# Norm sums with split operands, and three weight blocks in the front, in a one-core decoder layer

## The chip, the core and the metric

The kernel runs on one core of a Trainium2 chip. A core has five engines that matter here, each with its own instruction queue, worked off in order: TensorE (PE, matrix products, with PEld for the load of the stationary operand), VectorE (DVE), ScalarE (ACT), GpSimd (POOL) and SyncE (SP), which here only starts transfers. Transfers between the chip's main memory and the core's own memory run on 16 DMA engines. The metric is the device time of one execution in microseconds, the median of several runs; smaller is better.

Two number formats appear. f32 is full single precision. f32r is a 32-bit format of reduced precision that TensorE takes at its ordinary rate. Writing a value x to an f32r tile rounds it (the high part, `hi`); `lo` is x - `hi`, written to another f32r tile. A product of two numbers is then taken as hi*hi + hi*lo + lo*hi, three f32r matmuls.

## The reference

One layer of a decoder for 256 prompt positions and 8 x 4 sample positions, 288 columns in all, with d_model 2048 and d_ff 5632. Cut to what matters:

```python
z = einsum('ntd,de->nte', x, w_in)          # one input projection: h, Bg, Cg, q, k, v, two gates
ya = gate_b * conv3(gate_c * h)             # mixer A
yb = dilated_window_attention(q, k, v)      # mixer B, three head groups
mixed = sigmoid(g_a) * (ya @ w_branch_a) + sigmoid(g_b) * (yb @ w_branch_b)
x1 = layernorm(ALPHA * x + mixed @ w_out, ln1_g, ln1_b)
a, b = split(x1 @ w_up)
y = layernorm(ALPHA * x1 + (silu(conv3(a)) * b) @ w_down, ln2_g, ln2_b)
```

The layer norm takes mean and variance over the 2048 features of each position. Features lie on the 128 partitions, 16 blocks of them, and positions along a row, so a sum over features is a sum over 16 blocks and then over partitions; the latter is a matmul with a matrix of equal entries.

## The kernel before

**Products.** Every weight matrix is cut into blocks of 128 output features: 128 partitions by 16 k-slices of 128, 1 MB in f32. `prepare()` loads the next block of `weight_list()` into one of three `wst` buffers by an SP transfer (L167), and `half_block` splits it in two halves of eight k-slices: ScalarE casts the high part to `whi` (L138), VectorE subtracts for `wlo` (L139); there are four buffers of each. `product(x)` takes a prepared block and issues for each k three matmuls into an accumulator of 288 columns (L208 to L210), 48 in all. There are five accumulators (`acc`). The order of instructions on each engine is made by a scheduler, except where `behind(a, b)` puts a behind b.

**The front.** While the inputs arrive there is nothing to multiply with, so the first two blocks of `w_in` (0 and 1) are handled apart. `FIRST` cuts the 16 k-slices into six pieces: four of two and two of four. For each piece one transfer brings its x slices (288 or 576 KB; the first four on ScalarE's queue, the others on SP's; L242) and one the same k of both blocks (256 or 512 KB, SP, L243). `split` makes high and low parts of both (L214 on ScalarE, L215 on VectorE). `first_two()` prepares block 2 by `prepare()` and multiplies piece by piece: for each piece the terms hi*hi, hi*x-low and lo*hi, over the piece's k and both blocks (L262). Then block 2 follows as an ordinary product. A warm-up of 18 matmuls on zeros (L227) runs ahead of all that. SP's transfers of the front wait for an earlier one by a semaphore: eight are under way at a time.

**The norm.** `Norm` keeps two running sums, s1 of the values and s2 of their squares. `first()` runs after feature block 0: a matmul with `ones_p` (1/128 everywhere, L610) gives the mean of block 0 for each position, which is copied to `c` (L611) and subtracted from all blocks, so that s1 and s2 stay small. `add(i)` squares a block on ScalarE (L618) and adds it to the sums on GpSimd (L622, L623). For the last block it does not add: two matmuls with `ones_d` (1/2048) take s1 and s2 (L630), and two more take the last block and its square into the same accumulators (L631). All of these ones-matmuls are in f32. `finish()` for norm 1 then forms mean and 1/r on ScalarE and VectorE (L639 to L647). The products that follow the first norm start on values that aren't normalized yet; `normed` (L712 to L715) applies 1/r to their result, so TensorE need not wait for it, but the accumulators are released only then. `finish_out()` for norm 2 is the tail of the kernel.

Of the kernel before, what the change touches and what calls it, by code (L numbers as in the profile page):

```python
# [11 lines left out]
F32R = mybir.dt.float32r  # L12
AF = mybir.ActivationFunctionType
ALU = mybir.AluOpType
# [3 lines left out]
P = 128  # L18
D = 2048
KD = D // P  # L20
# [3 lines left out]
T = SEQ + NS  # L24


H = T // 2
# [4 lines left out]
HK = KD // 2  # L32
# [24 lines left out]
R_LN = R_WCF + KF * 3  # L57
# [4 lines left out]
NB_QKV = 3 * NG * NH  # L62
# [21 lines left out]
def layer_kernel(ctx: ExitStack, tc: tile.TileContext, ins, outs):  # L84
    nc = tc.nc
    pe, dve, act, pool, sp = nc.tensor, nc.vector, nc.scalar, nc.gpsimd, nc.sync

    big = ctx.enter_context(tc.tile_pool(name="big", bufs=1))
    wp = ctx.enter_context(tc.tile_pool(name="wp", bufs=3))
    wk = ctx.enter_context(tc.tile_pool(name="wk", bufs=2))  # L90
# [4 lines left out]
    def nm(s):  # L95
        uid[0] += 1
        return f"{s}_{uid[0]}"

    def sb(pl, shape, tag, dt=F32, bufs=None):
        return pl.tile(shape, dt, tag=tag, name=nm(tag), bufs=bufs)  # L100

    def acc(half=H):
        return sb(ps, [P, half, 2], "acc")
# [4 lines left out]
    def h3(ap):  # L108
        return ap.rearrange("p k (h a) -> p k h a", h=2)

    def att(cols=512):
        return sb(ps, [P, cols], "att", bufs=2)

    def f32(ap):
        return ap.bitcast(F32)
# [9 lines left out]
    def behind(i, after):  # L125

        tc.add_manual_dep(i.ins, after.ins.name, no_sync, reason="pace")
# [12 lines left out]
        return hi, lo, n  # L140

    def weight_list():
        for b in range(2, NB_QKV + 3 * KD):
            yield ins["w_in"][b], KD
        for gate, w, nk in ((0, "w_a", KD), (KD, "w_b", NH)):
            for i in range(KD):
                yield ins["w_in"][NB_QKV + 3 * KD + gate + i], KD
                yield ins[w][i], nk
        for i in range(KD):
            yield ins["w_out"][i], KD  # L150
        f = wd = 0
        for nf in THIRDS:
            for _ in range(2 * nf):
                yield ins["w_up"][f], KD
                f += 1
            for _ in range(KD):
                yield ins["w_down"][wd : wd + nf * P * P].rearrange("(p c) -> p c", p=P), nf
                wd += nf * P * P

    w_left = weight_list()  # L160

    def prepare():
        src, nk = next(w_left, (None, 0))
        if nk == 0:
            return
        st = sb(wp, [P, KD, P], "wst")
        d = sp.dma_start(st[:, :nk, :], src.rearrange("p (k c) -> p k c", c=P))  # L167
        loads[0] += 1
        n = loads[0]
        w_load[0] = d  # L170
        if n > NB_QKV + 5 * KD and n % 11 in (0, 4, 8):
            copy_rest(d)
        w_ready.append([half_block(st, k0, min(HK, nk - k0)) for k0 in range(0, nk, HK)])
# [13 lines left out]
    def product(x):  # L187

        w = w_ready.pop(0)
        if not w_ready:  # L190
            prepare()
        if steps_on[0]:
            spent[0] += N_STEP
            while spent[0] >= N_STEP_BLOCKS:
                spent[0] -= N_STEP_BLOCKS
                next(steps, None)
        o = acc(x[0].shape[-1])
        mms(o, w, x)
        prompt_step()
        return o.rearrange("p a h -> p h a")  # L200
# [10 lines left out]
                k += 1  # L211

    def split(hi, lo, src):
        act.copy(hi, src)  # L214
        dve.tensor_tensor(lo, src, f32(hi), ALU.subtract)  # L215

    ones_d = sb(big, [P, P], "ones_d")
    ones_p = sb(big, [P, P], "ones_p")
    pool.memset(ones_d, 1.0 / D)
    pool.memset(ones_p, 1.0 / P)  # L220


    zero = sb(wk, [P, T], "cy", F32R, bufs=2)
# [1 line left out]
    o = sb(ps, [P, T], "acc")  # L225
# [4 lines left out]
    xh = sb(big, [P, KD, 2, HX], "xh", F32R)  # L230
    xl = sb(big, [P, KD, 2, HX], "xl", F32R)
    x_in = ins["x"].rearrange("p (k t) -> p k t", t=T)
    xs = sb(big, [P, KD, T], "yah")

    w_ready = []
    w_two = sb(big, [P, 2, KD, P], "dd")
    w_two_hi = sb(big, [P, 2, KD, P], "yal", F32R)
    w_two_lo = [sb(wk, [P, 2, HK, P], "cache", F32R, bufs=2) for _ in range(2)]
    w_in_two = ins["w_in"][0:2].rearrange("b p (k c) -> p b k c", c=P)
    for k0, n, queue in FIRST:  # L240
        k = slice(k0, k0 + n)
        (act if queue == "act" else sp).dma_start(xs[:, k], x_in[:, k])  # L242
        sp.dma_start(w_two[:, :, k], w_in_two[:, :, k])  # L243
    for k0, n, _ in FIRST:
        k = slice(k0, k0 + n)
        split(xh[:, k, :, :H], xl[:, k, :, :H], h3(xs[:, k]))
        split(w_two_hi[:, :, k], w_two_lo[k0 // HK][:, :, k0 % HK : k0 % HK + n], w_two[:, :, k])
    x = (xh[:, :, :, :H], xl[:, :, :, :H])
    x_gb = (xh[:, :, :, :HG], xl[:, :, :, :HG])

    def first_two():

        prepare()
        o = [acc() for _ in range(2)]
        before = None
        for k0, n, _ in FIRST:
            for term in range(3):
                for k in range(k0, k0 + n):
                    xk = x[term == 1][:, k].rearrange("p h a -> p a h")
                    for b in range(2):  # L260
                        w = w_two_lo[k // HK][:, b, k % HK] if term == 2 else w_two_hi[:, b, k]
                        i = pe.matmul(  # L262
                            o[b], w, xk, start=k == 0 and term == 0, stop=k == KD - 1 and term == 2
                        )
                        if before is not None:
                            behind(i, before)
                        before = i
        return [t.rearrange("p a h -> p h a") for t in o]
# [37 lines left out]
    def prompt_attention(j, qT, kT, vT):  # L306
# [46 lines left out]
        ])  # L353
        act.copy(oT, po)
        split(ybh[:, j, :SEQ], ybl[:, j, :SEQ], oT)


# [27 lines left out]
    def pick_t(out, p, add):  # L385

        for t in range(NT):
            dve.scalar_tensor_tensor(
                out, p[:, t * P : (t + 1) * P], tmask[:, t : t + 1], add if t == 0 else out, ALU.mult, ALU.add
            )  # L390
# [94 lines left out]


    kv = sb(big, [P, 2, 2, NG, T], "dd")
    q_first = first_two()
    for j in range(NH):
        for g in range(NG):  # L490
            act.copy(h2(q_all[:, j, g]), q_first.pop(0) if q_first else product(x))
            if j == 1:
                dst, src = ((cst, ins["cst"][:, :C_M0]), (m_dist, ins["cst"][:, C_M0:]), (prm, ins["prm"]))[g]
# [58 lines left out]
    for i in range(KD):  # L552
        ph = product(x)
        h = sb(wk, [P, T], "h", bufs=2)
# [12 lines left out]
        ya = sb(wk, [P, T], "ya", bufs=2)  # L567
# [6 lines left out]
    for i in range(KD):  # L574
# [3 lines left out]
        o = product((h3(yah), h3(yal)))  # L578
# [6 lines left out]
    for i in range(KD):  # L585
# [3 lines left out]
        o = product((h3(ybh), h3(ybl)))  # L589
# [6 lines left out]
    dd = sb(big, [P, KD, T], "dd")  # L596

    lw = sb(wk, [P, 7, T], "cache", bufs=2)

    class Norm:  # L600


        def __init__(self, g, b):
            self.g, self.b = g, b
            self.s1, self.s2, self.c = (lw[:, k] for k in range(3))

        def first(self):

            p = att(T)
            pe.matmul(p, ones_p, dd[:, 0], start=True, stop=True)  # L610
            act.copy(self.c, p)  # L611
            dve.tensor_tensor(dd[:, 0], dd[:, 0], self.c, ALU.subtract)

        def add(self, i):
            d = dd[:, i]
            last = i == KD - 1
            q = self.s2 if i == 0 else sb(wk, [P, T], "cy", bufs=2)
            act.activation(q, d, AF.Square)  # L618
            if i == 0:
                pool.tensor_copy(self.s1, d)  # L620
            elif not last:
                pool.tensor_tensor(self.s1, self.s1, d, ALU.add)  # L622
                pool.tensor_tensor(self.s2, self.s2, q, ALU.add)  # L623
            if i == KD - 2:

                act.activation(lw[:, 3, 0:1], q[:, 0:1], AF.Abs_reciprocal_sqrt)
            if last:
                self.p1, self.p2 = att(T), att(T)
                for p, s, e in ((self.p1, self.s1, d), (self.p2, self.s2, q)):
                    pe.matmul(p, ones_d, s, start=True, stop=False)  # L630
                    pe.matmul(p, ones_d, e, start=False, stop=True)  # L631

        def at(self, c, i):
            return prm[:, c + i : c + i + 1]
# [51 lines left out]
                sp.dma_start(out[:, k0 : k0 + n, :], y[:, k0 : k0 + n, :])  # L686


    n1 = Norm(R_LN, R_LN + KD)
    for i in range(KD):  # L690
        o = product((h3(mxh), h3(mxl)))
        xf = sb(wk, [P, T], "h", bufs=2)
# [25 lines left out]

    cf = sb(big, [P, KF, 2 + 2 * NB], "qk_s")
    f = 0  # L720
    n2 = Norm(R_LN + 2 * KD, R_LN + 3 * KD)
    for part, nf in enumerate(THIRDS):
        gh = sb(big, [P, KD, T], "yah", F32R)
        gl = sb(big, [P, KD, T], "yal", F32R)
# [30 lines left out]
        for i in range(KD):  # L755
            o = product((h3(gh), h3(gl)))
# [197 lines left out]
```

## Time and profile before

| | us |
|---|---|
| median of 3 runs | 1764.37 (1764.05 to 1764.5) |
| the profiled execution's own time | 1764.45 |
| its span, first to last instruction | 1762.7 |
| TensorE busy | 1744.4 |
| VectorE, ScalarE, GpSimd busy | 1008.0, 797.3, 254.1 |
| moved by DMA | 436.25 MB, mean 247 GB/s |
| granted TensorE clock, mean | 0.997 |

In the rows of the profile "start us, us, engine line op out<-in xcount" tells when an instruction (or a run of equal ones) began, how long it lasted, which engine and which line of the program it belongs to, and what it wrote from what; in brackets stands how long its engine was idle before it and what released it. TensorE's matmuls overlap one another, so the distance between two starts, not the printed 0.29 us, is what one takes. In a row of a window ("from:to length, ...") stand the busy time and count of PE, PEld, DVE, ACT and POOL, the granted clock, the share of the DMA engines in use and GB/s. A row of the waits has the total, the number and the longest. A row of transfers has count, size and median time from issue to landing.

### The profile page before, as it was taken

The numbers are of one execution on the slowest core, as the hardware profiler recorded it, in microseconds if no ns is written. First come the engines' busy times: TensorE is split into PE (matmuls) and PEld (weight loads), VectorE is DVE, ScalarE is ACT, GpSimd is POOL, SyncE is SP. The second block draws the span as 40 slices with busy tenths as digits, with TensorE's granted clock in tenths as the row PEclk, the third lists the DMA queues.
The fourth block names the chain that finished last, engine by engine and source line by source line (L and its number), as shares of the span: only waits on it lengthen the run. The fifth ranks groups of instructions, "written<-read, shape, count | busy, mean of one in ns | idle before, by whom it ended". The sixth has DMA issues, their size and how long they took to land.

```text
span 1762.7 us, 33587 instructions
## 1 busy us (share of the span) xinstructions
PE 1744.4 (99%) x14275; PEld 1713.7 (97%) x14275; DVE 1008.0 (57%) x1317; ACT 797.3 (45%) x1167; POOL 254.1 (14%) x401
## 2 busy tenths in 40 slices
PE   9999999999999999999999999999999999999996
PEld 9999999999999999999999999999999999999996
DVE  5444455555555444455588788774555554555564
ACT  5444444333434333344455655553444443345444
POOL 0000000000000000001155233310011110011174
PEclk9999999999999999999999999999999999999998
DMA  8477787787787887467766566656565666666653
GB/s 325 173 287 266 270 299 297 266 324 295 273 332 282 306 314 264 150 247 260 282 233 221 220 230 217 237 216 236 218 237 218 236 219 234 220 234 221 237 198 108
DMA packets 60198, 436.25 MB, mean 247 GB/s; under 512 B 7184, under 2 KB 8336, under 8 KB 16016
## 3 DMA queue, kind: packets, MB, share of 16 engines
q1 hardware_dynamic: 58320, 429.40, 66.2%
q10 hardware_dynamic: 1728, 4.72, 0.7%
q8 instruction: 111, 1.82, 0.4%
q14 instruction: 39, 0.32, 0.0%
HBM read 389.89 MB, written 94.53 MB: 275 GB/s over the span
## 4 chain that ended last, share of the span: by engine, by line
PE 97%; DMA 1%; ACT 1%; DVE 1%; POOL 0%; issue 0%; SPq 0%; ACTq 0%; DVEq 0%
PE acc L208 31%; PE acc L209 31%; PE acc L210 31%; PE long L407 1%; PE long L460 1%; DMA wst<-in_w_in 1%; PE att L348 0%; DMA dd<-in_w_in 0%; PE att L312 0%; ACT whi L138 0%; POOL qk_s L535 0%; ACT yah L685 0%; DVE dd L661 0%; ACT xh L214 0%; PE att L340 0%; PE att L332 0%
## 5 line engine op out<-in xcount | busy, mean ns | idle before, releaser
L139 DVE TENSOR_TENSOR wlo<-wst,whi 128x1024 fp32r<-128x1024 f32 (+1 forms) x580 | 711.1, 1227 | 617.8 <-ACT whi L138 610.8
L138 ACT CAST whi<-wst 128x1024 fp32r<-128x1024 f32 (+1 forms) x580 | 592.0, 1022 | 877.1 <-PE acc L209 769.5
L208 PE MATMUL acc<-xh,whi 128*128 128x288 f32 (+1 forms) x3232 | 928.0, 287 | 0.0
L210 PE MATMUL acc<-xh,wlo 128*128 128x288 f32 (+1 forms) x3232 | 925.4, 286 | 0.1
L209 PE MATMUL acc<-xl,whi 128*128 128x288 f32 (+1 forms) x3232 | 925.0, 286 | 0.0
L208 PEld LDWEIGHTS acc<-xh,whi 128*128 128x128 f32 x3232 | 610.8, 189 | 8.0 <-ACT cy L519 2.5
L210 PEld LDWEIGHTS acc<-xh,wlo 128*128 128x128 f32 x3232 | 610.8, 189 | 1.2 <-issue 0.8
L209 PEld LDWEIGHTS acc<-xl,whi 128*128 128x128 f32 x3232 | 610.9, 189 | 0.4 <-issue 0.2
L208 PE MATMUL acc<-yah,whi 128*128 128x288 f32 x1216 | 348.2, 287 | 0.3 <-ACT yah L214 0.3
L210 PE MATMUL acc<-yah,wlo 128*128 128x288 f32 x1216 | 347.8, 286 | 0.0
L209 PE MATMUL acc<-yal,whi 128*128 128x288 f32 x1216 | 347.6, 286 | 0.0
L208 PEld LDWEIGHTS acc<-yah,whi 128*128 128x128 f32 x1216 | 229.7, 189 | 3.2 <-ACT h L577 2.5
L210 PEld LDWEIGHTS acc<-yah,wlo 128*128 128x128 f32 x1216 | 229.8, 189 | 0.1
L209 PEld LDWEIGHTS acc<-yal,whi 128*128 128x128 f32 x1216 | 229.8, 189 | 0.1
L535 POOL COPY qk_s<-u 128x2 f32<-128x2 f32 x44 | 41.8, 949 | 573.7 <-ACT u L735 441.5
L521 DVE SCALAR_TENSOR_TENSOR cy<-u,prm,cy 128x304 f32<-128x304 f32 x120 | 70.7, 589 | 3.1 <-ACT cy L519 0.4
L592 POOL TENSOR_TENSOR ya<-ya,dd 128x288 f32<-128x288 f32 x16 | 13.6, 852 | 306.0 <-DVE ya L591 306.0
L546 DVE TENSOR_TENSOR ya<-cy,acc 128x144 f32<-128x144 f32 x132 | 25.6, 249 | 33.6 <-PE acc L210 33.6
L535 POOL COPY cm<-u 128x2 f32<-128x2 f32 x16 | 3.0, 187 | 254.1 <-DVE u L560 254.1
L214 ACT CAST yah<-ya 128x288 fp32r<-128x288 f32 x76 | 32.7, 431 | 14.0 <-POOL ya L592 8.8
L215 DVE TENSOR_TENSOR yal<-ya,yah 128x288 fp32r<-128x288 f32 x76 | 34.9, 459 | 1.3 <-ACT yah L214 1.2
L622 POOL TENSOR_TENSOR cache<-cache,dd 128x288 f32<-128x288 f32 x28 | 27.7, 988 | 46.6 <-DVE dd L701 31.5
(166 smaller groups left out, 812.4 us busy)
## 6 DMA issues: line engine op xcount, KB each, us to landing
wst<-in_w_in SPq DMA_DIRECT2D x114, 1024.0 KB, 6.0
wst<-in_w_up SPq DMA_DIRECT2D x88, 1024.0 KB, 4.8
wst<-in_w_down SPq DMA_DIRECT2D x32, 1024.0 KB, 4.9
cache<-in_ck SPq DMA_DIRECT2D x18, 1024.0 KB, 6.4
out_o_ck<-cache SPq DMA_DIRECT2D x18, 1024.0 KB, 9.3
cache<-in_cv SPq DMA_DIRECT2D x18, 1024.0 KB, 6.3
out_o_cv<-cache SPq DMA_DIRECT2D x18, 1024.0 KB, 9.9
wst<-in_w_a SPq DMA_DIRECT2D x16, 1024.0 KB, 4.9
```

The lines of the kernel that those rows point to most:

```text
L138: act.copy(hi[:, :n, :], st[:, k0 : k0 + n, :])
L139: dve.tensor_tensor(lo[:, :n, :], st[:, k0 : k0 + n, :], f32(hi[:, :n, :]), ALU.subtract)
L208: pe.matmul(out, hi[:, c, :], xh_k, start=k == 0, stop=False)
L209: pe.matmul(out, hi[:, c, :], xl_k, start=False, stop=False)
L210: last_mm[0] = pe.matmul(out, lo[:, c, :], xh_k, start=False, stop=k == nk - 1)
L214: act.copy(hi, src)
L215: dve.tensor_tensor(lo, src, f32(hi), ALU.subtract)
L407: row.append(pe.matmul(p[j * NS : (j + 1) * NS], qm[:, j, b, :], c[:, o + j * cols : o + (j + 1) * cols], start=b == 0, stop=b == NB - 1,))
L521: dve.scalar_tensor_tensor(y, u[:, i : i + YW], prm[:, w0 + i : w0 + i + 1], y, ALU.mult, ALU.add)
L535: pool.tensor_copy(dst[:, 0:2], u[:, SEQ : SEQ + 2])
L546: dve.tensor_tensor(a, b, c, ALU.mult)
L622: pool.tensor_tensor(self.s1, self.s1, d, ALU.add)
```

## The change

Two edits that do not touch one another.

The front takes three blocks instead of two. Block 2 gets a `wst` buffer of its own and two `whi` and `wlo` buffers, as it would have had from `prepare()`, but it is loaded in the same six pieces, a transfer of 128 or 256 KB behind each piece of blocks 0 and 1, and split piece by piece. `first_three()` multiplies all three blocks within each term. The splits' order (x, blocks 0 and 1, block 2, piece after piece) is fixed on ScalarE and on VectorE by `behind`. `prepare()`, called at the head of it, now loads block 3.

The norm's matrices of ones are stored as f32r. `first()` casts block 0 to f32r first and multiplies the high part alone. In norm 1 (`tail` False) `add` puts the last block into s1 and s2 as well, splits both sums at once (a cast and a subtract of 128 x 576) and issues four f32r matmuls, high parts and then low parts. Norm 2 (`tail` True) keeps its four f32 matmuls on the last block.

```diff
-        for b in range(2, NB_QKV + 3 * KD):
+        for b in range(3, NB_QKV + 3 * KD):
...
     def split(hi, lo, src):
-        act.copy(hi, src)
-        dve.tensor_tensor(lo, src, f32(hi), ALU.subtract)
-
-    ones_d = sb(big, [P, P], "ones_d")
-    ones_p = sb(big, [P, P], "ones_p")
-    pool.memset(ones_d, 1.0 / D)
-    pool.memset(ones_p, 1.0 / P)
+        return act.copy(hi, src), dve.tensor_tensor(lo, src, f32(hi), ALU.subtract)
+
+    ones_d = sb(big, [P, P], "ones_d", F32R)
+    ones_p = sb(big, [P, P], "ones_p", F32R)
+    pool.memset(f32(ones_d), 1.0 / D)
+    pool.memset(f32(ones_p), 1.0 / P)
...
+    w_one = sb(wp, [P, KD, P], "wst")
+    w_one_hi, w_one_lo = ([sb(wp, [P, HK, P], n, F32R, bufs=4) for _ in range(2)] for n in ("whi", "wlo"))
+    w_in_one = ins["w_in"][2].rearrange("p (k c) -> p k c", c=P)
     for k0, n, queue in FIRST:
         k = slice(k0, k0 + n)
         (act if queue == "act" else sp).dma_start(xs[:, k], x_in[:, k])
         sp.dma_start(w_two[:, :, k], w_in_two[:, :, k])
+        sp.dma_start(w_one[:, k], w_in_one[:, k])
+    splits = []
     for k0, n, _ in FIRST:
         k = slice(k0, k0 + n)
-        split(xh[:, k, :, :H], xl[:, k, :, :H], h3(xs[:, k]))
-        split(w_two_hi[:, :, k], w_two_lo[k0 // HK][:, :, k0 % HK : k0 % HK + n], w_two[:, :, k])
+        splits.append(split(xh[:, k, :, :H], xl[:, k, :, :H], h3(xs[:, k])))
+        h = slice(k0 % HK, k0 % HK + n)
+        splits.append(split(w_two_hi[:, :, k], w_two_lo[k0 // HK][:, :, h], w_two[:, :, k]))
+        splits.append(split(w_one_hi[k0 // HK][:, h], w_one_lo[k0 // HK][:, h], w_one[:, k]))
+    for before, after in zip(splits, splits[1:]):
+        for i in range(2):
+            behind(after[i], before[i])
...
-    def first_two():
+    def first_three():
 
         prepare()
-        o = [acc() for _ in range(2)]
+        o = [acc() for _ in range(3)]
+
+        def first_w(lo, b, k):
+            if b < 2:
+                return w_two_lo[k // HK][:, b, k % HK] if lo else w_two_hi[:, b, k]
+            return (w_one_lo if lo else w_one_hi)[k // HK][:, k % HK]
...
-                    for b in range(2):
-                        w = w_two_lo[k // HK][:, b, k % HK] if term == 2 else w_two_hi[:, b, k]
+                    for b in range(3):
                         i = pe.matmul(
-                            o[b], w, xk, start=k == 0 and term == 0, stop=k == KD - 1 and term == 2
+                            o[b], first_w(term == 2, b, k), xk, start=k == 0 and term == 0, stop=k == KD - 1 and term == 2
                         )
...
         def first(self):
 
+            hi = sb(wk, [P, T], "ya", F32R, bufs=2)
+            act.copy(hi, dd[:, 0])
             p = att(T)
-            pe.matmul(p, ones_p, dd[:, 0], start=True, stop=True)
+            pe.matmul(p, ones_p, hi, start=True, stop=True)
...
-            elif not last:
+            elif not last or not self.tail:
                 pool.tensor_tensor(self.s1, self.s1, d, ALU.add)
                 pool.tensor_tensor(self.s2, self.s2, q, ALU.add)
...
-                for p, s, e in ((self.p1, self.s1, d), (self.p2, self.s2, q)):
-                    pe.matmul(p, ones_d, s, start=True, stop=False)
-                    pe.matmul(p, ones_d, e, start=False, stop=True)
+                if self.tail:
+                    for p, s, e in ((self.p1, self.s1, d), (self.p2, self.s2, q)):
+                        pe.matmul(p, f32(ones_d), s, start=True, stop=False)
+                        pe.matmul(p, f32(ones_d), e, start=False, stop=True)
+                else:
+                    w = sb(wk, [P, 4, T], "cache", F32R, bufs=2)
+                    split(w[:, 0:2], w[:, 2:4], lw[:, 0:2])
+                    for k in range(4):
+                        pe.matmul((self.p1, self.p2)[k % 2], ones_d, w[:, k], start=k < 2, stop=k >= 2)
...
-    n1 = Norm(R_LN, R_LN + KD)
+    n1 = Norm(R_LN, R_LN + KD, False)
...
-    n2 = Norm(R_LN + 2 * KD, R_LN + 3 * KD)
+    n2 = Norm(R_LN + 2 * KD, R_LN + 3 * KD, True)
```

More of the change, by code (lines that the diff above doesn't have):

```diff
@@ L487, in layer_kernel @@
     kv = sb(big, [P, 2, 2, NG, T], "dd")
-    q_first = first_two()
+    q_first = first_three()
     for j in range(NH):
@@ L600, in layer_kernel, with __init__ @@
     class Norm:
-        def __init__(self, g, b):
-            self.g, self.b = g, b
+        def __init__(self, g, b, tail):
+            self.g, self.b, self.tail = g, b, tail
             self.s1, self.s2, self.c = (lw[:, k] for k in range(3))
         def first(self):
+            hi = sb(wk, [P, T], "ya", F32R, bufs=2)
+            act.copy(hi, dd[:, 0])
             p = att(T)
-            pe.matmul(p, ones_p, dd[:, 0], start=True, stop=True)
+            pe.matmul(p, ones_p, hi, start=True, stop=True)
             act.copy(self.c, p)
```

## The prediction

> **What bounds the kernel now.** I read the page's engine rows first, then the chain that ended last, then TensorE's waits, then the order of time at the two places that the edit touches.
>
> ```profile
> span 1762.7 us, 33587 instructions
> PE 1744.4 (99%) x14275; PEld 1713.7 (97%) x14275; DVE 1008.0 (57%) x1317; ACT 797.3 (45%) x1167; POOL 254.1 (14%) x401
> PE 97%; DMA 1%; ACT 1%; DVE 1%; POOL 0%; issue 0%; SPq 0%; ACTq 0%; DVEq 0%
> PE acc L262 <- ACT yal L214: 1.2, 2, 0.7
> PE acc L208 <- ACT yah L214: 0.3, 1, 0.3
> 26.32:1745.34 1719.02, 1718.67 (x14107) 1690.22 (x14105) 982.25 (x1284) 772.42 (x1129) 245.28 (x387) 1.00 0.67 247
> ```
>
> TensorE sets the end: 97% of the chain is its matmuls, and the last row, a window from 26.32 to 1745.34 us, shows it busy for 1718.67 of 1719.02 us at granted clock 1.00, DMA engines 67% used. A matmul taken out of that window shortens the run by its own length, and so does an earlier start of the window; VectorE (57%), ScalarE (45%) and GpSimd (14%) count only where TensorE waits for them. It waits at the front:
>
> ```profile
> 5.01 0.67 ACT L214 CAST xh<-yah 128x576 fp32r<-128x576 f32 x1 [0.96 <-DMA yah<-in_x]
> 6.26 0.76 PE L262 MATMUL acc<-xh,yal 128*128 128x288 f32 x4 [0.74 <-ACT yal L214]
> 8.18 0.75 DVE L215 TENSOR_TENSOR xl<-yah,xh 128x576 fp32r<-128x576 f32 x1
> 12.97 1.05 ACT L214 CAST yal<-dd 128x1024 fp32r<-128x1024 f32 x1 [0.16 <-DMA dd<-in_w_in]
> 14.06 1.25 PE L262 MATMUL acc<-xh,yal 128*128 128x288 f32 x8 [0.42 <-ACT yal L214]
> 15.73 1.05 ACT L214 CAST yal<-dd 128x1024 fp32r<-128x1024 f32 x1 [0.16 <-DMA dd<-in_w_in]
> 18.23 2.00 ACT L138 CAST whi<-wst 128x1024 fp32r<-128x1024 f32 x2 [1.45 <-DMA wst<-in_w_in]
> 20.05 0.29 PE L208 MATMUL acc<-xh,whi 128*128 128x288 f32 x1
> 20.58 0.39 PE L210 MATMUL acc<-xh,wlo 128*128 128x288 f32 x1
> 20.81 0.29 PE L208 MATMUL acc<-xh,whi 128*128 128x288 f32 x1
> 22.27 1.99 ACT L138 CAST whi<-wst 128x1024 fp32r<-128x1024 f32 x2 [1.45 <-DMA wst<-in_w_in]
> 26.32 0.29 PE L208 MATMUL acc<-xh,whi 128*128 128x288 f32 x1
> ```
>
> Blocks 0 and 1 run from 6.26 to 20.05, block 2 from 20.05 to 26.32, where block 3 begins. From 20.81 to 26.32 are 15 k of three matmuls: 5.51 / 45 = 0.1224 us a matmul. Three blocks are 144 matmuls, 17.63 us; back to back from 6.26 they would end at 23.89. So 26.32 - 23.89 = 2.43 us of idle TensorE is all that the front can give.
>
> **The change, the norm.** The rows show a true f32 ones-matmul between ordinary ones, at the first and at the last feature block of norm 1:
>
> ```profile
> 876.50 0.46 DVE L695 SCALAR_TENSOR_TENSOR dd<-h,acc 128x288 f32<-128x288 f32 x1 [0.30 <-PE acc L210]
> 879.11 0.29 PE L210 MATMUL acc<-yah,wlo 128*128 128x288 f32 x1
> 879.24 0.65 PE L610 MATMUL att<-dd,ones_p 128*128 128x288 f32 x2
> 879.51 0.50 PE L208 MATMUL acc<-yah,whi 128*128 128x288 f32 x1
> 879.84 0.29 PE L209 MATMUL acc<-yal,whi 128*128 128x288 f32 x1
> 964.86 0.29 PE L210 MATMUL acc<-yah,wlo 128*128 128x288 f32 x1
> 964.98 1.13 PE L630 MATMUL att<-cache,ones_d 128*128 128x288 f32 x4
> 966.07 0.29 PE L209 MATMUL acc<-xl,whi 128*128 128x290 f32 x1
> 1679.65 0.45 DVE L763 TENSOR_TENSOR dd<-dd,acc 128x288 f32<-128x288 f32 x1
> 1682.38 0.65 PE L610 MATMUL att<-dd,ones_p 128*128 128x288 f32 x2
> ```
>
> From 879.11 to 879.84 pass 0.73 us, with one f32 matmul beside two ordinary steps: 0.73 - 0.245 = 0.485. From 964.86 to 966.07, two of them: (1.21 - 0.245) / 2 = 0.483. The edit turns six into f32r: one in each norm's first(), four in norm 1's last add (norm 2's last keeps f32). Removed 6 x 0.483 = 2.90, added 6 x 0.1224 = 0.73: **2.17 us** saved. No row shows a ones-matmul in f32r; the bounds are the price of L209, f32r of the same 128x288 shape (saves 2.17), and that of L610 (saves 0). I take L209, whose operands have the new type.
>
> Added around them: in first() one ScalarE copy (0.40 us, the L611 row below), and at norm 1's last block two GpSimd adds, a cast of 128x576 (0.67, the 5.01 row) and a subtract (0.75, the 8.18 row).
>
> ```profile
> 959.90 0.80 POOL L622 TENSOR_TENSOR cache<-cache,dd 128x288 f32<-128x288 f32 x1 [2.37 <-DVE dd L701]
> 961.19 1.24 POOL L623 TENSOR_TENSOR cache<-cache,cy 128x288 f32<-128x288 f32 x1 [0.49 <-ACT cy L618]
> 965.18 0.45 DVE L701 TENSOR_TENSOR dd<-h,acc 128x288 f32<-128x288 f32 x1 [0.42 <-PE acc L210]
> 966.45 0.43 ACT L618 ACTIVATE cy<-dd 128x288 f32<-128x288 f32 x1
> 973.16 0.46 DVE L647 SCALAR_TENSOR_TENSOR cache<-cache 128x288 f32<-128x288 f32 x1
> 975.14 0.45 DVE L714 TENSOR_TENSOR h<-acc,cache 128x288 f32<-128x288 f32 x1
> 880.31 0.39 ACT L611 COPY cache<-att 128x288 f32<-128x288 f32 x1
> 1157.04 4.42 POOL L535 COPY qk_s<-u 128x2 f32<-128x2 f32 x1 [9.72 <-ACT u L731]
> ```
>
> They hide if the sums are ready when TensorE comes to them. The square ends at 966.88, the second add about 968.2, the cast 968.9, the subtract 969.7. In the changed program's order of instructions the pair on the high half stands 47 matmuls into the first up-projection, 964.98 + 47 x 0.123 = 970.8, and the pair on the low half five ordinary matmuls later, 971.6: 1.9 us of cover each. Without it the overrun is paid in full. In first() block 0's sum ends at 876.96 in norm 1 and 1680.10 in norm 2 (rows of L695 and L763), 2.3 us ahead of L610, whose successor stands six and four matmuls later still; the 0.40 us copy fits in. One ScalarE weight cast (1.05) waits behind it, for a block wanted a product later. Cost 0.
>
> Late next is 1/r (973.62 at the end of L647): the matmuls end 1.8 us later, and in VectorE's new order a weight subtract stands ahead of the variance step and another inside the chain; I estimate L714 at 977.8 instead of 975.14. Behind the cast on ScalarE wait the two casts of the block that TensorE needs at 977, and behind the chain on VectorE those of the block needed at 983 (48 x 0.123 = 5.9 us a product); five accumulators hold the products until then. So 2.7 us later costs nothing; the same delay beyond 983 would.
>
> **The change, the front.** Block 2 no longer comes as one 1 MB transfer after the others but as six, each behind the same k of x and blocks 0, 1. The bytes to its end are the same, 5.5 MB, so its last should land near 18.23 as now. Piece 5 (k 8 to 11) decides: now it is complete at 12.97, and 0.79 MB of block 2 come ahead of its end.
>
> ```profile
> 6.26:14.06 7.80, 7.08 (x48) 6.14 (x48) 6.08 (x9) 5.78 (x8) 0.00 (x0) 1.00 1.04 396
> 14.06:20.05 5.99, 5.99 (x49) 5.99 (x49) 4.51 (x5) 4.02 (x4) 0.00 (x0) 1.00 1.04 423
> wst<-in_w_a SPq DMA_DIRECT2D x16, 1024.0 KB, 4.9
> wst<-in_w_b SPq DMA_DIRECT2D x16, 256.0 KB, 2.7
> ```
>
> At 396 to 423 GB/s that is 1.9 to 2.0 us: landed about 14.9, after the pair's cast (1.05, begun at 14.3) the third's (estimated 0.6, half of 1.05 and a start) ends at 16.0. TensorE comes to piece 5 at 6.26 + 72 x 0.1224 = 15.1 plus the stalls of the early pieces, 0.72 us now (7.08 busy of 7.80). From 16.0 there are 72 matmuls, less the two on blocks 0 and 1 that go ahead: 16.0 + 70 x 0.1224 = 24.6. Piece 6 lands by 18.3, its casts end by 19.4, TensorE needs it at 20.3. So block 3 begins at 24.6 and the front gives **1.7 us**, bounds 0 (feed again last) and 2.43.
>
> The added splits, 6 casts and 6 subtracts of 256 or 512 columns, replace two and two of 1024: more starts, same elements. The order that is now written out makes each wait for its piece; behind a late one stand the next x's. SP issues 14 transfers ahead of block 3 where 9 stood, and each waits for one some eight earlier: block 3's issue slips from about 9.4 to 12, but its bytes were queued until 22.27 anyway. Its split (1.05 + 1.23) is then ready at 24.6, its first low-half matmul wanted at 24.85: cover 0.25 us, and each us that it lands later costs nearly one. Blocks 4 and 5 have 5.9 us more each.
>
> **Sum.** 2.17 + 1.7 = 3.87 us off the profiled 1764.45 (span 1762.7 and 1.75 around it), 0.08 above the median: 1764.37 - 3.87 = **1760.5**.
>
> **The rivals.**
> *The front stays feed-bound* (12%): smaller pieces move slower than 396 GB/s; at 10% less, the 13 us of feeding up to piece 5 take 1.4 more, and the front gives 0.3: 1764.37 - 2.17 - 0.3 = 1761.9. For it: the casts at 12.97 and 15.73 ended waits for DMA. Against: 256 KB pieces already ran in the 396 window.
> *Norm 1's sums are late* (6%): GpSimd once takes 4.42 us for a copy of two columns; an add 3.5 us long overruns the 1.9 of cover by 1.6: 1762.1. Against: the adds' own rows, 0.80 and 1.24.
> *The ones-matmuls are no faster in f32r* (5%): only the front is left, 1762.7. Against: L209's step.
> *Slower: the six pieces add their fixed times one after another* (5%). By the last two rows 0.75 MB make 4.9 - 2.7 = 2.2 us, so 2.7 us for 256 KB and 2.3 for 128 KB: 2 x 2.7 + 4 x 2.3 = 14.6 against 4.9, 9.7 us more ahead of block 3. 1764.37 - 3.87 + 9.7 = 1770.2. It decides once over 3.9 of the 9.7 us aren't hidden. Against: two blocks and x, 4.46 MB in 14 smaller transfers, were all in by 15.73, which transfers in series would not be.
> The Trainium skill speaks for this rival: "DMA: Bandwidth & Descriptors", sections on the anatomy of one DMA and on bandwidth, has about 2.0 us fixed plus bytes at 436 GB/s for each (measured on GpSimd's path) and asks for 1 MiB batches. By it the six take 14.4 us against 4.4, and the time would be 1770.5. The trace does not agree for transfers in flight together, 396 GB/s in pieces of 256 to 576 KB.
>
> **How the numbers follow.** 72% for the forecast, with its own range 1760.0 to 1761.4 (front 0.8 to 2.2). The rivals hold the other 28%. The range 1759.8 to 1762.3 takes in the dense front and the first two rivals. By the bound of 0.2% (3.5 us, about what a measurement of this kernel can tell from no change), faster means below 1760.84: three quarters and more of the forecast, 56%. Within: the rest of it and three rivals, 39%. Slower: 5%.
>
> **What would show it.** Right: block 3's first matmul near 24.6 with no gap behind it, casts of piece 5 ending near 16, ones-matmuls one ordinary step apart, no TensorE wait from 970 to 985, span near 1759. Wrong: a gap before block 3 or piece 6 (feed), a TensorE wait for the sums' cast, an early piece's wait over 1 us.

## The result, and the profile after

| | us |
|---|---|
| before, median of 22 runs | 1764.07 (1763.84 to 1764.5) |
| changed, median of 22 runs | 1761.7 (1761.37 to 1763.11) |
| ratio | 0.9987, 95% interval 0.9981 to 0.9993 |
| changed, profiled execution | 1763.11, the longest of its 22; span 1761.3 |

The change takes off 2.37 us, 0.13%, where 3.87 were forecast. The ratio's interval excludes 1, yet the gain is under the 0.2% (3.5 us) that the prediction set as its bound for "faster". Of the 22 times, 18 lie within 1761.37 to 1761.75; the others are 1762.0, 1762.45, 1762.68 and 1763.11. The profile is of the last, so two things must be kept apart in it: what every execution has, and what only this tail has.

First the page's engine rows of the changed kernel, its waits of TensorE (total, number, longest), and a window from block 3's first matmul to the end (length, then busy time and count of PE, PEld, DVE, ACT, POOL, granted clock, DMA share, GB/s):

```profile
span 1761.3 us, 33600 instructions
PE 1743.9 (99%) x14269; PEld 1714.4 (97%) x14269; DVE 1008.2 (57%) x1322; ACT 798.4 (45%) x1174; POOL 254.8 (14%) x403
```
```profile
PE acc L226 <- DVE cy L223: 1.2, 1, 1.2
PE acc L210 <- DVE wlo L139: 0.6, 1, 0.6
PE acc L208 <- ACT yah L214: 0.3, 1, 0.3
PE acc L276 <- ACT yal L214: 0.2, 1, 0.2
```
```profile
26.28:1744.05 1717.77, 1716.83 (x14100) 1688.79 (x14099) 982.43 (x1285) 773.76 (x1134) 245.99 (x389) 1.00 0.67 247
```

Before, this window was 1719.02 us long with 0.35 us of it idle. Now it is 1717.77 with 0.94 idle. It was to lose the norm's 2.17 us and lost 1.25. The second wait, L210 on VectorE's low half of a weight block (L139), did not exist before. The front's waits of 1.2 us for ScalarE's casts (L262 before, L276 now) have shrunk to 0.2, and still block 3 begins at 26.28 where it began at 26.32. The timeline of the changed kernel's front says why:

```profile
6.12 0.85 PE L276 MATMUL acc<-xh,yal 128*128 128x288 f32 x2 [0.21 <-ACT yal L214]
...
9.25 0.45 PE L276 MATMUL acc<-xl,whi 128*128 128x288 f32 x1
9.49 0.69 PE L276 MATMUL acc<-xh,cache 128*128 128x288 f32 x2
9.97 0.45 PE L276 MATMUL acc<-xh,wlo 128*128 128x288 f32 x1
...
11.09 0.29 PE L276 MATMUL acc<-xh,whi 128*128 128x288 f32 x1
...
11.46 0.29 PE L276 MATMUL acc<-xh,whi 128*128 128x288 f32 x1
...
26.28 0.29 PE L208 MATMUL acc<-xh,whi 128*128 128x288 f32 x1
```

Read the distances between starts. From 9.25 to 9.97 are three matmuls, 0.24 us each; from 11.09 to 11.46 are three as well, 0.123 each. Up to 10.69 TensorE works at half speed, and no wait shows it, because the engine counts as busy there. The windows of the two stretches:

```profile
7.81:10.69 2.88, 2.88 (x14) 2.88 (x13) 1.70 (x4) 1.92 (x5) 0.00 (x0) 1.00 1.10 338
11.09:26.28 15.19, 15.19 (x126) 15.19 (x125) 11.40 (x15) 10.10 (x14) 0.00 (x0) 1.00 1.02 396
```

Both are wholly busy and both print a granted clock of 1.00. That column does not tell them apart, because the trace's entries of the clock begin only at 10.75 us, and time without an entry is counted as 1.00. At 10.75 the step falls from 0.24 to 0.123 us; the warm-up ahead of the front ran at 0.24 too. The Trainium skill, "TensorE: Matmul & The Clock Gate", section "What's actually happening", describes such a thing: matmuls pass at half rate until TensorE has been busy through a window of about 3.4 us, and since that window runs free, the moment of the change differs from run to run. The two steps here, 0.24 and 0.123 us, agree with the half rate; the length of the window is shown by no run.

Then the place of the new wait, the start of a product in norm 2, in the timeline of the kernel before and of the changed one. The first row of each is GpSimd's run of subtractions of c; then come a square and the next weight cast on ScalarE, the low half on VectorE with GpSimd's adds beside it, and TensorE's first matmuls of the product that needs it:

```profile
1683.54 15.64 POOL L762 TENSOR_TENSOR dd<-dd,cache 128x288 f32<-128x288 f32 x14 [13.41 <-ACT cache L611]
...
1703.05 0.44 ACT L618 ACTIVATE cy<-dd 128x288 f32<-128x288 f32 x1 [1.76 <-POOL cache L623]
1703.40 1.55 ACT L138 CAST whi<-wst 128x1024 fp32r<-128x1024 f32 x2
...
1704.47 1.23 DVE L139 TENSOR_TENSOR wlo<-wst,whi 128x1024 fp32r<-128x1024 f32 x1 [2.10 <-PE acc L210]
1704.49 1.86 POOL L622 TENSOR_TENSOR cache<-cache,dd 128x288 f32<-128x288 f32 x1
...
1705.77 0.29 PE L208 MATMUL acc<-yah,whi 128*128 128x288 f32 x1
...
1706.02 0.29 PE L210 MATMUL acc<-yah,wlo 128*128 128x288 f32 x1
```
```profile
1681.88 15.96 POOL L785 TENSOR_TENSOR dd<-dd,cache 128x288 f32<-128x288 f32 x14 [13.56 <-ACT cache L628]
...
1701.25 0.44 ACT L635 ACTIVATE cy<-dd 128x288 f32<-128x288 f32 x1 [1.06 <-POOL cache L640]
1701.60 1.55 ACT L138 CAST whi<-wst 128x1024 fp32r<-128x1024 f32 x2
...
1702.67 1.90 DVE L139 TENSOR_TENSOR wlo<-wst,whi 128x1024 fp32r<-128x1024 f32 x1 [5.48 <-ACT whi L138]
1702.69 0.80 POOL L639 TENSOR_TENSOR cache<-cache,dd 128x288 f32<-128x288 f32 x1
1703.45 1.77 POOL L640 TENSOR_TENSOR cache<-cache,cy 128x288 f32<-128x288 f32 x1
...
1703.62 0.29 PE L208 MATMUL acc<-yah,whi 128*128 128x288 f32 x1
1703.74 0.29 PE L209 MATMUL acc<-yal,whi 128*128 128x288 f32 x1
1704.62 0.39 PE L210 MATMUL acc<-yah,wlo 128*128 128x288 f32 x1 [0.60 <-DVE wlo L139]
1704.85 0.29 PE L208 MATMUL acc<-yah,whi 128*128 128x288 f32 x1
```

Set both against the product's first matmul, 1705.77 and 1703.62. Before, the low half is done at 1705.70 and wanted at 1706.02: a cover of 0.32 us. Now it is wanted 0.245 us behind the first matmul, at 1703.86, and done at 1704.57: 0.71 late. The 1.03 us between come from two places. The subtract begins 0.95 us ahead of the product's start instead of 1.30, 0.35 later, and it takes 1.90 us instead of 1.23, 0.67 longer. From 1703.74 to 1704.85 TensorE makes two steps in 1.11 us, so 0.87 are lost; the 0.60 in brackets is the part put down to VectorE.

GpSimd's adds show where the 0.67 us lie. Before, the subtract took 1.23 and the add beside it 1.86. Now the add beside its start takes 0.80, the subtract 1.90 and the next add 1.77; the five adds ahead of them, with VectorE idle, took 0.79 to 0.80 each. Both lengths were there before: the three subtracts of this shape that began at 1696.68, 1704.47 and 1707.56 took 1.85, 1.23 and 1.84. So a long subtract is nothing new; it now falls where the cover is small.

Why it begins later can be followed upward. Its cast stands behind a square, and the square's buffer is freed by GpSimd's adds (L640), which stand behind the subtractions of c. These now end at 1697.84, 5.78 us ahead of the product; before, at 1699.18, 6.59 ahead. The order behind them differs too: now the fifteenth subtraction (1698.16) stands ahead of the first sum of squares (1698.92), before it stood behind it (1700.26, the sum at 1699.52). The adds that follow take less time than before, so that of the 0.81 us between 6.59 and 5.78 the subtract's start keeps 0.35.

### The profile page after: what moved, and what is told of

The parts are those of the page before. It is cut to its first block, busy times and chain, and to the rows that moved or that the text cites. A ratio compares the mean times of both kernels' runs of the same rounds, so it can differ in the third digit from the quotient of the medians.

```text
span 1761.3 us, 33600 instructions
## 1 busy us (share of the span) xinstructions
PE 1743.9 (99%) x14269; PEld 1714.4 (97%) x14269; DVE 1008.2 (57%) x1322; ACT 798.4 (45%) x1174; POOL 254.8 (14%) x403
## 4 chain that ended last, share of the span: by engine, by line
PE 96%; POOL 1%; ACT 1%; DVE 1%; issue 0%; DMA 0%; ACTq 0%; DVEq 0%
PE acc L208 31%; PE acc L210 31%; PE acc L209 31%; PE acc L276 1%; PE long L421 1%; PE long L474 1%; POOL dd L785 1%; PE att L362 0%; PE att L326 0%; ACT whi L138 0%; POOL qk_s L549 0%; ACT xh L214 0%; ACT yah L708 0%; DVE dd L684 0%; DMA yah<-in_x 0%
## 5 line engine op out<-in xcount | busy, mean ns | idle before, releaser
L139 DVE TENSOR_TENSOR wlo<-wst,whi 128x1024 fp32r<-128x1024 f32 (+1 forms) x578 | 706.9, 1224 | 617.3 <-ACT whi L138 613.2
L210 PE MATMUL acc<-xh,wlo 128*128 128x288 f32 (+1 forms) x3216 | 920.5, 286 | 0.0
L210 PEld LDWEIGHTS acc<-xh,wlo 128*128 128x128 f32 x3216 | 607.8, 189 | 0.8 <-issue 0.8
L210 PE MATMUL acc<-yah,wlo 128*128 128x288 f32 x1216 | 347.7, 286 | 0.6 <-DVE wlo L139 0.6
L210 PEld LDWEIGHTS acc<-yah,wlo 128*128 128x128 f32 x1216 | 229.8, 189 | 0.8 <-DVE wlo L139 0.8
```

The lines of the kernel that those rows point to most:

```text
L139: dve.tensor_tensor(lo[:, :n, :], st[:, k0 : k0 + n, :], f32(hi[:, :n, :]), ALU.subtract)
L210: last_mm[0] = pe.matmul(out, lo[:, c, :], xh_k, start=False, stop=k == nk - 1)
```

## The experiments

Each of the eight versions ran 11 times, in two batches of four; the kernel before had medians of 1764.14 us (1763.82 to 1764.74, 33 runs) and 1764.01 (1763.78 to 1764.33, 33 runs) beside them.

**The front alone.** The changed kernel with the norm as it was:

```diff
-    ones_d = sb(big, [P, P], "ones_d", F32R)
-    ones_p = sb(big, [P, P], "ones_p", F32R)
+    ones_d = sb(big, [P, P], "ones_d")
+    ones_p = sb(big, [P, P], "ones_p")
...
-            pe.matmul(p, ones_p, hi, start=True, stop=True)
+            pe.matmul(p, ones_p, dd[:, 0], start=True, stop=True)
...
-    n1 = Norm(R_LN, R_LN + KD, False)
+    n1 = Norm(R_LN, R_LN + KD, True)
```

> The front's edit alone: three blocks and fixed splits; all ones-matmuls in f32 as before. Theory 'clock': the front gains about 1.6 us when TensorE's matmuls run at 0.122 us from the first piece on (block 3 begins near 24.7) and next to nothing when they take 0.24 us for the first 4 us, as in the profile of the change (26.28); so the runs spread over more than 1 us, between 1762.4 and 1764.1. Rival 'feed': the pieces come too late, block 3 begins near 26.3 with idle gaps of TensorE between pieces, all runs within 0.4 us of 1764. The forecast had 1762.4 (-1.7).

Measured: 1762.90 (1762.63 to 1763.61), ratio 0.9993, interval 0.9984 to 1.0002. The front is worth 1764.14 - 1762.90 = 1.24 us by the medians, though the interval takes in 1. There is no TensorE wait near 1704 in its profile. The times spread over 0.98 us, just under the 1 us that was expected. The profiled execution, at 1763.28 one of the two longest, has its step of 0.122 from 7.17 us on, and yet block 3 begins only at 25.18: it is late by gaps at pieces of the front and not by the clock.

**The norm alone.** The kernel before, with the norm's edits and the front of two blocks.

> The norm's edit alone; the front with two blocks. Theory 'stall in norm 2': six ones-matmuls save 2.17 us, and a wait of TensorE of about 0.75 us for a low half of weights near 1704 gives part of it back, as in the profile of the change: 1764.07 - 1.4 = 1762.7. Rival 'f32r saves less': no such wait, and the steps around the ones-matmuls are longer than 0.15 us. The forecast had 1761.9 (-2.17).

Measured: 1762.88 (1762.78 to 1763.41), 0.9993, 0.9984 to 1.0001: 1.26 us by the medians, and here too the interval takes in 1. The new wait is there without the new front; from its waits of TensorE, its timeline in norm 2, and the last matmul on a high part of block 2:

```profile
PE acc L210 <- DVE wlo L139: 0.6, 1, 0.6
```
```profile
1702.37 1.91 DVE L139 TENSOR_TENSOR wlo<-wst,whi 128x1024 fp32r<-128x1024 f32 x1 [5.49 <-ACT whi L138]
...
25.61 0.29 PE L208 MATMUL acc<-xh,whi 128*128 128x288 f32 x1
```

So the wait belongs to the norm edit. Three matmuls behind 25.61, at 25.98, this front of two blocks hands over to block 3: 0.34 us earlier than the 26.32 of the execution from which the prediction was made.

**A longer warm-up.** The changed kernel with 24 matmuls on zeros ahead of the front:

```diff
-N_WARM = 18
+N_WARM = 24
```

> The changed kernel with 24 warm-up matmuls in place of 18, so that TensorE is busy until the first piece is there. Theory 'clock': matmuls of the front take 0.122 us from the first piece or soon after, block 3 begins at 25 at the latest in the profile, no run above 1762.2, median 1761.5 or below. Rival 'feed': block 3 begins where it did or later, and the median does not fall.

Measured: 1761.72 (1761.64 to 1762.23), 0.9987, 0.9978 to 0.9995. The step is 0.122 us from the first piece (6.45) on, and block 3 begins early:

```profile
24.80 0.29 PE L208 MATMUL acc<-xh,whi 128*128 128x288 f32 x1
```

The expectation holds in part: block 3 begins early, but the median is that of the changed kernel and not 1761.5 or below, and four of the 11 times lie at 1762.05 to 1762.23, apart from the other seven. An unchanged median with the clock up says that the changed kernel's usual execution has its clock up as well. The times near 1763 are gone; only two of the changed kernel's 22 lay above 1762.5, though, so 11 times do not show that the longer warm-up took them away.

**Turns on GpSimd.** The changed kernel, with the subtraction of c for block i of norm 2 behind the sum of block i - 2:

```diff
-                pool.tensor_copy(self.s1, d)
+                self.sums = [None] * KD
+                self.sums[0] = pool.tensor_copy(self.s1, d)
...
-                pool.tensor_tensor(self.s2, self.s2, q, ALU.add)
+                self.sums[i] = pool.tensor_tensor(self.s2, self.s2, q, ALU.add)
...
-                    pool.tensor_tensor(dd[:, i], dd[:, i], n2.c, ALU.subtract)
+                    i_sub = pool.tensor_tensor(dd[:, i], dd[:, i], n2.c, ALU.subtract)
+                    if i > 2:
+                        behind(i_sub, n2.sums[i - 2])
```

> The changed kernel with GpSimd's work in norm 2 put in turns: the subtraction of c from block i waits until the square of block i-2 is added, so that fourteen subtractions no longer stand ahead of the first sums. Theory 'stall in norm 2': ScalarE's squares no longer wait 4 us for GpSimd, the weight casts behind them come in time, TensorE's wait near 1704 is gone, 0.75 us less than the change: about 1760.9. Rival 'the subtract itself is slowed by GpSimd': a wait of TensorE in that stretch stays, and the time with it (1761.7).

Measured: 1760.90 (1760.58 to 1762.33), 0.9982, 0.9974 to 0.9991. All of its waits of TensorE but the warm-up's, and its timeline in norm 2:

```profile
PE acc L276 <- ACT yal L214: 1.0, 2, 0.8
PE acc L208 <- ACT yah L214: 0.3, 1, 0.3
```
```profile
1699.44 0.45 ACT L635 ACTIVATE cy<-dd 128x288 f32<-128x288 f32 x1 [1.00 <-DVE dd L789]
...
1701.83 1.37 DVE L139 TENSOR_TENSOR wlo<-wst,whi 128x1024 fp32r<-128x1024 f32 x1 [1.88 <-ACT whi L138]
```

ScalarE's square now waits for its data (VectorE, L789) and no longer for GpSimd, the subtract takes 1.37 us, and the wait of L210 is gone. The median is 0.80 us below that of the changed kernel; by the kernel before beside each, it is 3.24 off instead of 2.37, 0.87 more.

**A shorter warm-up.** `N_WARM = 10` in the changed kernel.

> The changed kernel with 10 warm-up matmuls in place of 18: they end near 3.7, and TensorE idles until 6.1. Theory 'clock': the first pieces are multiplied at 0.24 us a matmul for some 3 to 4 us, block 3 begins at 26.2 or later, and the whole distribution moves up to where the slow tail of the change lies, median 1762.8 to 1763.3. Rival 'feed, not clock, sets the front': block 3 begins at 24.8 to 25.2 as in the fast runs, 1761.7.

Measured: 1763.05 (1762.23 to 1763.65), 0.9994, 0.9985 to 1.0003. From its front:

```profile
9.48 0.45 PE L276 MATMUL acc<-xl,whi 128*128 128x288 f32 x1
9.72 0.69 PE L276 MATMUL acc<-xh,cache 128*128 128x288 f32 x2
10.20 0.45 PE L276 MATMUL acc<-xh,wlo 128*128 128x288 f32 x1
```

Three matmuls take 0.72 us as in the tail of the changed kernel, block 3 begins at 26.78, and all 11 times lie at 1762.23 or above, where only three of that kernel's 22 do. So a shorter warm-up makes the rule of what is a tail with 18.

**The turns without the norm edit.** The front alone, with the turns: a control, to see whether the turns give anything where there is no wait to remove.

> The front's edit alone (norm in f32) with GpSimd's work in norm 2 in turns. Control for the run with turns: where there was no wait of TensorE in norm 2 the turns give nothing, so 1762.9 as for the front alone; if the turns gain by themselves, 1762.1.

Measured: 1762.81 (1762.70 to 1763.33), 0.9993, 0.9985 to 1.0002, against 1762.90 for the front alone in the other batch. They give nothing by themselves.

**Norm 2's first ones-matmul back in f32.** The changed kernel without the cast in `first()` of norm 2, and without the turns:

```diff
-            hi = sb(wk, [P, T], "ya", F32R, bufs=2)
-            act.copy(hi, dd[:, 0])
             p = att(T)
-            pe.matmul(p, ones_p, hi, start=True, stop=True)
+            if self.tail:
+                pe.matmul(p, f32(ones_p), dd[:, 0], start=True, stop=True)
+            else:
+                hi = sb(wk, [P, T], "ya", F32R, bufs=2)
+                act.copy(hi, dd[:, 0])
+                pe.matmul(p, ones_p, hi, start=True, stop=True)
```

> The changed kernel, but norm 2's first ones-matmul stays f32 without the cast of block 0, so that ScalarE's order in norm 2 is that of the kernel before. Theory 'stall in norm 2 comes with the cast in its first()': the wait near 1704 is gone, 0.75 less and 0.35 more for the f32 matmul: 1761.3. Rival 'it comes from the shift in time alone': the wait stays and 0.35 come on top: 1762.05.

Measured: 1761.11 (1760.95 to 1762.48), 0.9985, 0.9976 to 0.9994. Its waits of TensorE but the warm-up's, and the start of block 3:

```profile
PE acc L208 <- ACT yah L214: 0.3, 1, 0.3
PE acc L276 <- ACT yal L214: 0.2, 1, 0.2
PE acc L276 <- ACT whi L214: 0.2, 1, 0.2
```
```profile
24.71 0.29 PE L208 MATMUL acc<-xh,whi 128*128 128x288 f32 x1
```

Taking one matmul back to f32, 0.35 us dearer, made the kernel 0.59 us quicker (0.53 by the kernel before beside each), because the L210 wait goes with it. Two different edits, this and the turns, remove the wait, and the time falls with both. This one also puts GpSimd's order back to that of the kernel before (the first sum of squares at 1696.14, the fifteenth subtraction at 1696.89), so it does not tell the cast from the order that came with it. Its times also have a tail, four from 1761.91 to 1762.48, with 18 warm-ups.

**Both remedies.** Turns and a warm-up of 21.

> The changed kernel with GpSimd's work in norm 2 in turns and 21 warm-up matmuls, which reach to the first piece. Both theories: no wait in norm 2, no half-speed front: median 1760.8, no run above 1761.6. Rival: the longer warm-up delays the first piece, 1761.2 or more.

Measured: 1760.79 (1760.57 to 1761.67), 0.9982, 0.9974 to 0.9991; block 3 begins at 24.64 us. The bound of 1761.6 for the highest time was just missed. This is the version with the lowest median and the lowest highest time of all that ran.

**The ten profiled executions side by side.** "Clock from" is where the trace's entries of the granted clock begin; in each of the ten, TensorE's step is 0.24 us ahead of that point and 0.12 to 0.13 behind it. The last column is the execution's time less the start of block 3, so that it leaves the front out. All in us:

| | warm-ups | clock from | block 3 from | time | time less block 3's start |
|---|---|---|---|---|---|
| before | 18 | 4.92 | 26.32 | 1764.45 | 1738.13 |
| front alone | 18 | 5.97 | 25.18 | 1763.28 | 1738.10 |
| front and turns | 18 | 7.44 | 25.25 | 1763.33 | 1738.08 |
| norm alone | 18 | 6.88 | 25.98 | 1762.88 | 1736.90 |
| changed | 18 | 10.75 | 26.28 | 1763.11 | 1736.83 |
| changed, longer warm-up | 24 | 5.58 | 24.80 | 1761.65 | 1736.85 |
| changed, shorter warm-up | 10 | 11.54 | 26.78 | 1763.62 | 1736.84 |
| changed, norm 2's first in f32 | 18 | 5.75 | 24.71 | 1761.03 | 1736.32 |
| changed, turns | 18 | 4.63 | 24.77 | 1760.73 | 1735.96 |
| changed, both remedies | 21 | 4.69 | 24.64 | 1760.62 | 1735.98 |

The last column falls into groups that agree within 0.07 us: the norm edit takes off 1.25, the turns 0.88 more where the wait is and 0.02 where it isn't. Together 1.25 and 0.88 are 2.13, close to the 2.10 that the six cheaper ones-matmuls come to below. What else differs among these ten lies ahead of block 3.

## Why the prediction came out as it did

The range held the time. The point, 1760.5, was 1.2 us too low, and the gain 1.5 too large: the base of 1764.37 was a median of three runs, and with the 1764.07 of 22 the same sum gives 1760.2. The measured 1761.7 lies outside the forecast's own range of 1760.0 to 1761.4, among the times of two rivals (1761.9 and 1762.1). Neither rival's mechanism is what happened, so it is luck that the wide range held the time.

**TensorE as the bound: right.** Every difference found here is one in TensorE's idle, doubled or removed steps.

**The f32r ones-matmul: right.** The timeline of the changed kernel at norm 1's first and last block:

```profile
879.81 0.29 PE L210 MATMUL acc<-yah,wlo 128*128 128x288 f32 x1
879.93 0.29 PE L627 MATMUL att<-ya,ones_p 128*128 128x288 f32 x1
880.06 0.29 PE L208 MATMUL acc<-yah,whi 128*128 128x288 f32 x1
...
967.96 0.67 ACT L214 CAST cache<-cache 128x576 fp32r<-128x576 f32 x1 [1.48 <-POOL cache L640]
968.67 0.76 DVE L214 TENSOR_TENSOR cache<-cache,cache 128x576 fp32r<-128x576 f32 x1 [0.42 <-ACT cache L214]
970.38 0.43 PE L654 MATMUL att<-cache,ones_d 128*128 128x288 f32 x2
970.65 0.28 PE L210 MATMUL acc<-xh,wlo 128*128 128x290 f32 x1
971.27 0.42 PE L654 MATMUL att<-cache,ones_d 128*128 128x288 f32 x2
...
976.71 0.45 DVE L737 TENSOR_TENSOR h<-acc,cache 128x288 f32<-128x288 f32 x1
```

One takes 0.13 us (879.93 to 880.06), two take 0.27 (970.38 to 970.65). Six of them save 6 x (0.483 - 0.133) = 2.10 us, where 2.17 was forecast. The rival that f32r is no faster falls.

**Norm 1's sums: right.** The cast ends at 968.63 and TensorE comes at 970.38; the subtract ends at 969.43 and TensorE comes at 971.27. The cover is 1.75 and 1.84 us, forecast 1.9. No wait stands in the list there, and the rival of the late sums falls.

**1/r later at no cost: right.** VectorE comes to the first product after the norm (L737, L714 before) at 976.71 (forecast 977.8, before 975.14), 1.6 us later, and no wait of TensorE answers to it.

**"Cost 0" in first(): the step that failed.** In the time of block 0 itself all fits in, as forecast. But the step followed the copy only to the weight cast behind it, and not what hangs on c: GpSimd's 14 subtractions, behind them its sums, behind these ScalarE's squares, and behind a square the weight cast of a product 20 us on. At the end of that row of waits stood a cover of 0.32 us, which the prediction did not look for. Three things drew on it. GpSimd's run begins 1.66 us earlier than before (1683.54 to 1681.88) and ends 1.34 earlier (1699.18 to 1697.84), while TensorE, with the saved matmul, is 2.15 earlier (1705.77 to 1703.62). So the saving on TensorE is itself part of the lateness. And the subtract takes 0.67 us more. By the medians, the norm alone gave 1.26 of its 2.10, so 0.84 were lost, against 0.87 in the trace; the turns gave 0.80 back by the medians and 0.88 by the table.

That the wait hangs on norm 2's `first()` and on GpSimd's order behind it is shown by the two edits that remove it: the turns change that order, the other takes back the cast, the order that came with it and 0.35 us of TensorE's saving at once. The shares, 0.35 for the start and 0.67 for the subtract, are read from the two traces; neither was changed without the other. Why the subtract and GpSimd's run (15.96 us for 15.64) take longer stays open.

**The front: wrong size, and another piece decides.** Forecast were 1.7 us, block 3 going from 26.32 to 24.6. It does start at 24.64 to 24.80 in four versions with the clock up, so the feed-bound rival and the slower one, fixed times of the six pieces in series, fall. But piece 5, which was to decide, does not: in those four its casts end at 15.44 to 15.90, TensorE comes to it at 15.81 to 15.98, and it is wholly busy from 9.7 us to block 3. What TensorE lost, 0.72 to 0.95, it lost at the first two pieces. That the number fits is in part luck, since this path is about as long as the one foreseen: by the prediction's own terms 6.26 + 17.63 + 0.72 = 24.61. In the two versions that have this front without the norm edit piece 5's casts end at 16.44 and 16.52, TensorE does lose 0.13 and 0.32 us there, and block 3 begins at 25.18 and 25.25. (The front before has 12 smaller transfers for x and two blocks, not the 14 that the prediction counts; nothing hangs on it.)

What was off by more is the other end of the difference: 26.32 came from one execution, at 1764.45 longer by 0.38 than the median of 22, and the norm alone, with the same front, has 25.98. 25.98 less 24.75, the middle of those four, is 1.23, and the medians say 1.24. Piece 5's casts in the changed kernel:

```profile
14.82 1.05 ACT L214 CAST yal<-dd 128x1024 fp32r<-128x1024 f32 x1 [0.94 <-DMA dd<-in_w_in]
15.78 0.61 ACT L214 CAST whi<-wst 128x512 fp32r<-128x512 f32 x1
```

They end at 16.39, 0.4 later than the 16.0 worked out, and in this execution TensorE, late itself, did not feel it.

**What was not foreseen: the clock.** The prediction took 0.1224 us a matmul from 6.26 on. The trace before had steps of 0.24 in its warm-up up to 4.75, and the prediction did not ask when they end. In the slowest execution of the changed kernel the first 17 or so matmuls of the front run at that rate, and block 3 starts at 26.28, so that the front gives almost nothing. That the warm-up has to do with it is shown by the version with 10, all of whose times lie where only the tail did. It does not explain the whole tail: the other slow executions of the changed kernel have no profile, and those two, at 1763.28 and 1763.33, had the clock up by 7.44 us. Whether more than 18 warm-ups help stays open: the spread is 1.74 us with 18, 1.75 with 18 and the turns and 1.53 with norm 2's first in f32, but 0.98 and 0.63 for the same two; with 24 it is 0.59, with 21 and the turns 1.10.

**The sum.** 1.24 from the front and 1.26 from the norm make 2.50, measured 2.37. With the wait removed by the turns, 1.24 + 2.10 = 3.34, measured 1764.14 - 1760.90 = 3.24. The two edits add up, within 0.13 us.

## What to carry to other kernels

A step that is hidden where it stands must be followed along everything that waits for its result, to the smallest cover at the end of that row, and a saving on the bounding engine can shorten every such cover behind it, as it did here. A gain at the start of a kernel should be taken from several executions and not from one, since there a few tenths of a microsecond, and TensorE's clock, differ between them. A warm-up that ends well ahead of the first real matmul is too short: with 10 the median was 1.35 us longer than with 18; whether it has to reach all the way to that matmul was not settled here. And where only the start of a kernel differs between executions, the time less the start of the common part compares versions more finely than the medians do: here to 0.07 us.

## What the runs showed of the hardware that was not expected

- TensorE stepped at 0.24 us in place of 0.122 for 4.6 us of the front while the granted clock printed 1.00 (window 7.81 to 10.69). The trace has no entry of the clock before the change, and the column takes that for 1.00. With the same 18 warm-ups the change came at 4.63 to 10.75 us.
- Beside GpSimd's adds a subtract of 128x1024 on VectorE took 1.90 us in one place and 1.23 in another, where the add took 1.86 in place of 0.80; with the turns it took 1.37. The Trainium skill, "SBUF — State Buffer", section "SBUF: two separate sides", has VectorE and GpSimd share a port that one of them holds at a time. That one of the two is long by turns agrees with it, but no run here measured the port by itself.
- Six transfers of 128 and 256 KB in place of one of 1 MB, in flight with others, cost no bandwidth that can be seen: 396 GB/s from 11.09 to 26.28, where the front before had 396 and 423.
